# Attention stage of a two-layer fp32 hybrid block: hi products ahead of lo ones, an output-projection chunk between the last key transposes, the last biases loaded two steps ahead

## Chip, cores and metric

The kernel runs on 1 core of one Trainium2 chip. The metric is the device time of one execution in microseconds. Before the change it is 1264.56 us, the median of 3 runs (1263.3 to 1265.16).

## What is computed

A block of two layers works on 256 latent tokens and 256 context tokens of width 1024. Each layer is a half-step SwiGLU FFN, a token mixer and a second half-step FFN, and every one of these ends in a modulated, gated LayerNorm update. The mixer of layer 0, where the change is, is neighbourhood attention with 16 heads of 64: the latent queries see a window of the latent keys, with a relative bias and a mask, and all context keys, in one softmax.

```python
qkv = (hx @ w_qkv).reshape(B, S, 3, N_HEADS, HEAD_DIM)
q = apply_axial_rope(qkv[:, :, 0], rope)
k = apply_axial_rope(qkv[:, :, 1], rope)
v = qkv[:, :, 2]
...
s_win = jnp.where(mask, s_win + bias.astype(jnp.float32)[None], -jnp.inf)
s_ctx = jnp.einsum('bjqhd,bchd->bhjqc', q_r, k_c).astype(jnp.float32) * scale
p = jax.nn.softmax(jnp.concatenate([s_win, s_ctx], axis=-1), axis=-1).astype(v.dtype)
return (jnp.einsum('bhjqk,bjkhd->bjqhd', p[..., :nk], v_blk)
        + jnp.einsum('bhjqc,bchd->bjqhd', p[..., nk:], v_c))
...
y_lat = jnp.moveaxis(o, 0, 1).reshape(B, S, D) @ w_out
```

## The kernel before

**Hi and lo.** Every fp32 product is made of three. `split` (L110, L111) makes the hi part of a tile on ACT (a rounding copy) and then the lo part on DVE (source minus hi). A product of a and b is a_hi b_hi + a_hi b_lo + a_lo b_hi, with the three lines of `mmu` (L162, L163, L165) for the projections. A lo part is thus always ready one DVE instruction after its hi part.

**Who sets the order.** PE's instructions run in the order in which the program writes them. ACT, DVE, POOL and SP have their instructions placed by the tile framework's scheduler, from the same program and from priority offsets, so an edit of the program can move them too. Every engine takes its own list in order: an instruction that waits holds all behind it. Of the PSUM banks, transposes (`tpb`) share two, "mm" has three, "at" three.

**The attention stage** (about 465 to 585 us of the span). A loop of 32 steps goes over pairs of heads and two halves of the queries, `qt`. At every even step i, `scores` (L955 on) makes S for two heads at once (L962, three products for each), adds the bias tile (L966, DVE), takes the maximum (L968, DVE), the exponential (L970, ACT) and the scaling (L972, ACT), which gives `pr`. Two steps later `probs_T` transposes `pr` (L987, four 128x128 transposes into one bank PT) and splits the bank into pT hi and pT lo. One step after that, for the second half of the queries, `values` multiplies with v (L999 with the hi part, L1000 with the lo part, alternating, eight products) and sums into `osum` and `oT` (ACT and DVE).

**Fillers.** Between these, `fill_some` puts chunks of other products on PE: first the projections of keys, values and queries by quarters of the heads (`kv_quarter`, `q_half`), and from step 24 on the output projection `wo` of the heads that are done (`last_filler`). A wo chunk is one unit of six products; ten chunks are handed out by `islice(fin, 10)`, two of them of half a unit. The key transposes of a quarter (`rest`, L916 to L925) are two banks of four transposes, kT, and are made when a score needs them; those of the last quarter are made at step 24.

**Loads.** SP issues all loads of this stage in order. Each load waits until the one eight issues earlier has landed, and for its buffer. A bias tile takes two loads of 64 KB each (L874), from a table in which each row is read at another offset, and is then masked on POOL (L878). There are four bias buffers, and `bias_pair` for step i+2 is called at step i. The weights of the output projection, wor, come in 512 KB loads into four buffers that all projections share.

Of the kernel before, what the change touches and what calls it, by code (L numbers as in the profile page):

```python
# [9 lines left out]
F32 = mybir.dt.float32  # L10
# [6 lines left out]
P = 128  # L17
# [14 lines left out]
PB = {"mm": 3, "at": 3, "tp": 2}  # L32
W_EARLY = 40
ADA_SLOW, ADA_FAST = 3, 0.6
ADA_LATE = 20
ADA_LAG = 1
LN_EARLY = 60
# [31 lines left out]
def backbone_kernel(  # L69
# [6 lines left out]
    nc = tc.nc  # L76
# [9 lines left out]
    hp = phase.__enter__()  # L86
# [6 lines left out]
    def nm(s):  # L93
        uid[0] += 1
        return f"{s}_{uid[0]}"
# [10 lines left out]
    def tpb(s="tp"):  # L106
        return bank("tp", s)
# [358 lines left out]
    def run(gen):  # L466
        for _ in gen:
            pass
# [224 lines left out]
    steps = ((0, 1), (1, 1), (2, 2), (4, 2), (6, 2))  # L693
# [151 lines left out]
    def rtile(n):  # L845
        if n == 256:
            return hp.tile([P, n], F32, tag="kr", bufs=8, name=nm("kr"))
        return sp.tile([P, n], F32, tag="s2", bufs=S2, name=nm("qr"))
# [16 lines left out]

    BIAS = {}

    def bias_pair(h, qt):


        for hh in (h, h + 1):
            bt = hp.tile([P, 4, 64], F32, tag="bias", bufs=4, name=nm("bias"))
            for i in range(2):
                bias_dma[:] = [sync.dma_start(bt[64 * i:64 * i + 64],  # L874
                                              bass.AP(na_rpb_rev.tensor,
                                                      na_rpb_rev.offset + hh * 465 + (7 - 2 * qt - i) * 31 - 48,
                                                      [[1, 64], [31, 4], [1, 64]]))]
            nc.gpsimd.tensor_tensor(out=bt, in0=bt, in1=win_sb[:, ::-1].unsqueeze(1).to_broadcast([P, 4, 64]),  # L878
                                    op=ALU.add)
            BIAS[hh, qt] = bt[:, :, ::-1]  # L880
# [19 lines left out]
    def kv_quarter(g, res):  # L900
        krs, v = [], []

        def each(t, bk):
            if t < 2:
                krs.append(roped(bk[:, 0:256], t, 1, 4))
            else:
                r1 = rtile(256)
                nc.scalar.activation(r1, bk[:, 0:256], AF.Copy)
                krs.append(r1)
            v.append(act(F32R, "v"))  # L910
            z = v[t].rearrange("p (h s d) -> p h s d", h=4, s=2)
            split(bk[:, 256:512].rearrange("p (h d) -> p h d", h=4), z[:, :, 0], z[:, :, 1])

        yield from tile_panel(D + g * 256, 2 * D + g * 256, [hTs[t] for t in range(4)], "wkv", each)

        def rest():  # L916
            kT = []
            for j in range(2):
                ps = tpb("kT")
                for t in range(4):  # L920
                    nc.tensor.transpose(ps[:, t * P:(t + 1) * P], krs[t][:, j * P:(j + 1) * P], ident)
                hi, lo = act(F32R, "kTh"), act(F32R, "kTl")
                split(ps, hi, lo)
                kT.append((hi, lo))
            return kT  # L925

        res.append((Late(1, rest), v))
# [64 lines left out]
    def values(h):  # L992

        pth, ptl = PT.pop(h)
        ps = mmb("o", h == NH - 1)[:, 0:256]
        s = slice(h % 4 * P, (h % 4 + 1) * P)
        v = KV[h // 4][1]
        for k in range(4):
            nc.tensor.matmul(ps, v[k][:, s], pth[:, k], start=k == 0, stop=False)  # L999
            nc.tensor.matmul(ps, v[k][:, s], ptl[:, k], start=False, stop=k == 3)  # L1000
        if h % 2 == 0:
            osum[0] = sp.tile([P, 512], F32, tag="tmp", bufs=3, name=nm("osum"))[:, 0:256]
        p0 = h % 2 * 64
        t = osum[0][p0:p0 + 64]
        o_ins[h] = [nc.scalar.activation(t, ps[64:128], AF.Copy),
                    nc.vector.tensor_tensor(out=t, in0=ps[0:64], in1=t, op=ALU.add)]
        if h % 2:
            if len(oT) <= h // 4:
                oT.append([hp.tile([P, 512], F32R, tag="oT", bufs=6, name=nm("oT")) if len(oT) < 3 else act(F32R, "oT")
                           for _ in range(2)])  # L1010
            cs = slice((h // 2 % 2) * 256, (h // 2 % 2) * 256 + 256)
            last_o[:] = split(osum[0], *(z[:, cs] for z in oT[h // 4]))
# [34 lines left out]
    def fill_some(n):  # L1047
        for _ in range(n):
            if next(fill, 0) == 0:
                break  # L1050

    fill_some(A_PRE)
    for i in range(len(steps) + LAG + V_LAG):
# [4 lines left out]
                    sync.dma_start(xscr[t * P:(t + 1) * P, h * 512:(h + 1) * 512], xt[t][h])  # L1058
        while i + AHEAD < len(steps) and len(KV) <= steps[i + AHEAD][0] // 4:
            fill_some(1)  # L1060
        if i < len(steps) and i % 2 == 0:
            with tc.high_priority(offset=S_EARLY):
                prs[i], prs[i + 1] = scores(*steps[i])
            if i % 2 == 0 and i + 2 < len(steps):
                bias_pair(*steps[i + 2])
        credit += rate[min(i, len(rate) - 1)]
        n = int(credit)
        credit -= n
        if i >= 24 and fin is None:
            run(fill)  # L1070
            fin = last_filler()
            fill = islice(fin, 10)
        fill_some((n + 1) // 2)
        if i == len(steps) + LAG - 1:
            run(fill)
# [146 lines left out]
```

## Time and profile before

| | before |
|---|---|
| median of 3 runs | 1264.56 us (1263.3 to 1265.16) |
| profiled execution | 1262.04 us, span 1260.2 us |
| TensorE clock granted | full, in all 40 slices of the page |
| PE busy | 1242.7 us, 99% of the span |
| DVE, ACT, POOL busy | 950.1, 589.2, 41.5 us |
| chain that ended last | PE 90%, ACT 3%, DVE 3%, DMA 2% |

The profile is of one execution. In the timeline a line gives the start, the busy time, the engine, the line of the kernel, output and inputs, the number of instructions joined in the row, and in brackets the idle time ahead of it with the instruction that ended the idle time. Products on PE overlap, so the busy time of one is longer than the distance to the next start; distances of starts are used below.

### The profile page before, as it was taken

How to read it: one execution, taken by the hardware profiler on the slowest of the kernel's cores; microseconds unless marked ns; L12 is line 12 of the kernel's file. 1: busy time of each engine (PE TensorE's matmuls, PEld its weight loads, DVE VectorE, ACT ScalarE, POOL GpSimd, SP SyncE). 2: the span in 40 equal slices, each digit the busy share in tenths (PEclk: the TensorE clock that was granted, in tenths of full speed). 3: DMA queues.
4: the chain of work that ended last, by engine and by line, in shares of the span. 5: the costliest groups of instructions: out<-in, count | busy, mean ns of one | idle time of the engine just before them, and what ended most of it. 6: DMA issues, size and time to landing. Idle time of an engine off the chain costs nothing.

```text
span 1260.2 us, 17282 instructions
## 1 busy us (share of the span) xinstructions
PE 1242.7 (99%) x5910; PEld 1004.2 (80%) x5910; DVE 950.1 (75%) x1678; ACT 589.2 (47%) x1152; POOL 41.5 (3%) x71
## 2 busy tenths in 40 slices
PE   8999999999999999989999999999999999999997
PEld 5787778777878877867888788888788887888786
DVE  3699987888868877789889546988546788976546
ACT  2432132312326456687655435655435744655431
POOL 0000000000001111121000000000000000000000
PEclk9999999999999999999999999999999999999999
DMA  9976678788842744464899645898645764886641
GB/s 308 299 240 220 197 241 291 254 269 281 284 137 85 218 92 92 93 148 147 263 321 338 221 146 168 278 341 275 213 146 170 245 204 131 270 282 184 228 152 55
DMA packets 202776, 268.59 MB, mean 213 GB/s; under 512 B 30090, under 2 KB 149362, under 8 KB 202688
## 3 DMA queue, kind: packets, MB, share of 16 engines
q1 hardware_dynamic: 202652, 267.48, 67.2%
q8 instruction: 46, 0.75, 0.2%
q14 instruction: 42, 0.34, 0.1%
q10 hardware_dynamic: 36, 0.02, 0.0%
HBM read 265.27 MB, written 2.17 MB: 212 GB/s over the span
## 4 chain that ended last, share of the span: by engine, by line
PE 90%; ACT 3%; DVE 3%; DMA 2%; issue 1%; SPq 0%; POOL 0%; DVEq 0%; ACTq 0%
PE f L677 19%; PE w L162 17%; PE w L165 17%; PE w L163 17%; PE wkv L162 2%; PE wkv L163 2%; PE wkv L165 2%; PE wc L162 2%; PE wc L165 2%; PE wc L163 2%; PE gT L485 1%; DMA ar<-in_ada_w_dram 1%; PE ada L325 1%; PE hT L419 1%; PE S L962 1%
## 5 line engine op out<-in xcount | busy, mean ns | idle before, releaser
L208 ACT ACTIVATE w1h<-w1r 128x512 fp32r<-128x512 f32 (+1 forms) x352 | 199.9, 620 | 183.6 <-DMA w1r<-in_ffn_w_in_dram 63.5
L211 DVE TENSOR_TENSOR w1l<-w1r,w1h 128x512 fp32r<-128x512 f32 (+1 forms) x352 | 222.8, 678 | 49.2 <-ACT w1h L208 47.6
L162 PE MATMUL w<-w1h,hTh 128*128 128x512 f32 x528 | 209.4, 397 | 0.9 <-ACT hTh L110 0.9
L163 PE MATMUL w<-w1l,hTh 128*128 128x512 f32 x528 | 206.0, 390 | 0.2 <-DVE w1l L211 0.2
L294 DVE SCALAR_TENSOR_TENSOR acc<-ar,cst,acc 128x512 f32<-128x512 f32 x266 | 186.0, 745 | 14.5 <-DMA ar<-in_ada_w_dram 14.3
L162 PE MATMUL w<-w2h,gh 128*128 128x512 f32 (+1 forms) x446 | 173.4, 389 | 0.0
L163 PE MATMUL w<-w2l,gh 128*128 128x512 f32 (+1 forms) x446 | 172.1, 386 | 0.0
L211 DVE TENSOR_TENSOR w2l<-w2r,w2h 128x512 fp32r<-128x512 f32 x176 | 114.3, 687 | 76.3 <-ACT w2h L208 75.5
L208 ACT ACTIVATE w2h<-w2r 128x512 fp32r<-128x512 f32 x176 | 101.6, 624 | 145.4 <-PE w L165 101.6
L165 PE MATMUL w<-w1h,hTl 128*128 128x512 f32 x528 | 163.2, 390 | 0.3 <-DVE hTl L111 0.2
L165 PE MATMUL w<-w2h,gl 128*128 128x512 f32 (+1 forms) x446 | 136.0, 386 | 0.0
L677 PE MATMUL f<-h0h,w1h 128*128 128x512 f32 x352 | 132.8, 393 | 1.0 <-ACT w1h L208 0.6
L677 PE MATMUL f<-h0l,w1h 128*128 128x512 f32 x352 | 133.2, 391 | 0.0
L677 PE MATMUL f<-h0h,w1l 128*128 128x512 f32 x352 | 132.7, 390 | 0.0
L162 PEld LDWEIGHTS w<-w1h,hTh 128*128 128x128 f32 x528 | 99.2, 188 | 23.8 <-ACT hTh L110 1.7
L165 PEld LDWEIGHTS w<-w1h,hTl 128*128 128x128 f32 x528 | 98.9, 188 | 22.4 <-DVE hTl L111 1.5
L163 PEld LDWEIGHTS w<-w1l,hTh 128*128 128x128 f32 x528 | 99.2, 188 | 20.2 <-DVE w1l L211 0.6
L162 PEld LDWEIGHTS w<-w2h,gh 128*128 128x128 f32 x446 | 83.8, 188 | 19.3 <-issue 1.7
L163 PEld LDWEIGHTS w<-w2l,gh 128*128 128x128 f32 x446 | 83.8, 188 | 16.5
L165 PEld LDWEIGHTS w<-w2h,gl 128*128 128x128 f32 x446 | 83.3, 188 | 17.1
L677 PEld LDWEIGHTS f<-h0h,w1h 128*128 128x128 f32 x352 | 65.5, 188 | 19.4 <-issue 4.2
L677 PEld LDWEIGHTS f<-h0l,w1h 128*128 128x128 f32 x352 | 65.6, 188 | 14.3 <-issue 1.0
(184 smaller groups left out, 1697.3 us busy)
## 6 DMA issues: line engine op xcount, KB each, us to landing
w1r<-in_ffn_w_in_dram SPq DMA_DIRECT2D x340, 256.0 KB
ar<-in_ada_w_dram SPq DMA_DIRECT2D x128, 512.0 KB
w2r<-in_ffn_w_out_dram SPq DMA_DIRECT2D x88, 512.0 KB
ar<-in_ada_w_dram SPq DMA_DIRECT2D x32, 256.0 KB
wkvr<-in_na_w_qkv_dram SPq DMA_DIRECT2D x32, 256.0 KB
wcr<-in_sc_w_in_dram SPq DMA_DIRECT2D x32, 256.0 KB
wqr<-in_na_w_qkv_dram SPq DMA_DIRECT2D x8, 512.0 KB
bias<-in_na_rpb_dram SPq DMA_DIRECT2D x64, 64.0 KB
```

What stands on the lines that cost most here:

```text
L162: nc.tensor.matmul(ps, lh, rh, start=first and i == 0, stop=False)
L163: nc.tensor.matmul(ps, lh, rl, start=False, stop=False)
L165: nc.tensor.matmul(ps, ll, rh, start=False, stop=last and i == n - 1)
L208: nc.scalar.activation(hi[:, a:a + m // W_HI], raw[:, a:a + m // W_HI], AF.Copy)
L211: nc.vector.tensor_tensor(out=lo[:, a:b], in0=raw[:, a:b], in1=hi[:, a:b].bitcast(F32), op=ALU.subtract)
L294: nc.vector.scalar_tensor_tensor(out=a, in0=src, scalar=sc, in1=a, op0=ALU.mult, op1=ALU.add)
L325: nc.tensor.matmul(ps[32 * j:32 * j + 32, :], ones, acc[i][h], start=True, stop=True)
L419: nc.tensor.transpose(ps[:, k * P:(k + 1) * P], z[h][:, k * P:(k + 1) * P], ident)
L485: nc.tensor.transpose(ps[:, j * 256 + i * P:j * 256 + (i + 1) * P], g[:, j * P:(j + 1) * P], ident)
L677: nc.tensor.matmul(ps, w, hT0[k][part == 1], start=(k == part == 0), stop=(k == KC - 1 and part == 1))
L962: nc.tensor.matmul(banks[i], (qh, qh, ql)[f][ps, qs], (kh, kl, kh)[f][ps, :], start=f == 0, stop=f == 2)
```

## The change

The diff, with the two helpers' other lines cut:

```diff
+BIAS_AT = 24
...
-    def bias_pair(h, qt):
+    def bias_pair(h, qt, last=False):
         for hh in (h, h + 1):
-            bt = hp.tile([P, 4, 64], F32, tag="bias", bufs=4, name=nm("bias"))
+            if last:
+                bt = rtile(256).rearrange("p (a b) -> p a b", a=4)
+            else:
+                bt = hp.tile([P, 4, 64], F32, tag="bias", bufs=4, name=nm("bias"))
...
         def rest():
             kT = []
             for j in range(2):
+                if j and g == 3:
+                    fill_some(1)
                 ps = tpb("kT")
...
-        for k in range(4):
-            nc.tensor.matmul(ps, v[k][:, s], pth[:, k], start=k == 0, stop=False)
-            nc.tensor.matmul(ps, v[k][:, s], ptl[:, k], start=False, stop=k == 3)
+        for part, p in enumerate((pth, ptl)):
+            for k in range(4):
+                nc.tensor.matmul(ps, v[k][:, s], p[:, k], start=k == part == 0, stop=part == 1 and k == 3)
...
+        if i == BIAS_AT:
+            bias_pair(*steps[i + 2])
+            bias_pair(*steps[i + 4], True)
+            run(fill)
+            fin = last_filler()
+            fill = islice(fin, 10)
         if i < len(steps) and i % 2 == 0:
             with tc.high_priority(offset=S_EARLY):
                 prs[i], prs[i + 1] = scores(*steps[i])
-            if i % 2 == 0 and i + 2 < len(steps):
-                bias_pair(*steps[i + 2])
+        if i % 2 == 0 and i != BIAS_AT and (j := i + (2 if i < BIAS_AT else 4)) < len(steps):
+            bias_pair(*steps[j], i > BIAS_AT)
         credit += rate[min(i, len(rate) - 1)]
         n = int(credit)
         credit -= n
-        if i >= 24 and fin is None:
-            run(fill)
-            fin = last_filler()
-            fill = islice(fin, 10)
         fill_some((n + 1) // 2)
```

1. `values` makes its four products with the hi part first, then the four with the lo part, for all 16 heads.
2. Between the two banks of key transposes of the last quarter stands one wo chunk. For this the output projection is opened ahead of the scores of step 24. Ten chunks are handed out as before, so each later chunk moves one place forward.
3. The biases of step 28 are loaded at step 24 and those of step 30 at step 26, into tiles of the "kr" kind (the roped keys' buffers, of which there are eight), whose first use is over, in place of the "bias" buffers.

**The order on PE at the last key transposes** (step 24). PT and kT are banks of transposes, S the scores, wo the output projection, oT its left side. Before:

```order
L987 MATMUL PT_5180<-ident,pr_5075 128x128 x4
L921 MATMUL kT_5187<-ident,kr_4815 128x128
L921 MATMUL kT_5187<-ident,kr_4882 128x128
L921 MATMUL kT_5187<-ident,kr_4960 128x128
L921 MATMUL kT_5187<-ident,kr_5093 128x128
L921 MATMUL kT_5196<-ident,kr_4815 128x128
L921 MATMUL kT_5196<-ident,kr_4882 128x128
L921 MATMUL kT_5196<-ident,kr_4960 128x128
L921 MATMUL kT_5196<-ident,kr_5093 128x128
L962 MATMUL S_5205<-kTh_5192,qTh_4781 128x512
L962 MATMUL S_5206<-kTh_5192,qTh_4781 128x512
L962 MATMUL S_5205<-kTl_5193,qTh_4781 128x512
```

With the change:

```order
L927 MATMUL kT_5203<-ident,kr_4815 128x128
L927 MATMUL kT_5203<-ident,kr_4882 128x128
L927 MATMUL kT_5203<-ident,kr_4960 128x128
L927 MATMUL kT_5203<-ident,kr_5093 128x128
L163 MATMUL wo_5237<-woh_5230,oT_4327 128x512
L164 MATMUL wo_5237<-wol_5231,oT_4327 128x512
L163 MATMUL wo_5237<-woh_5230,oT_4327 128x512
L164 MATMUL wo_5237<-wol_5231,oT_4327 128x512
L166 MATMUL wo_5237<-woh_5230,oT_4328 128x512 x2
L927 MATMUL kT_5244<-ident,kr_4815 128x128
L927 MATMUL kT_5244<-ident,kr_4882 128x128
L927 MATMUL kT_5244<-ident,kr_4960 128x128
```

What moved: six wo products stand between the two kT banks, and no longer behind the scores; the scores follow the second bank at once in both.

**The order on PE at the end of the loop.** woh and wol are hi and lo of one unit of output weights, o the value sums. Before:

```order
L987 MATMUL PT_5549<-ident,pr_5415 128x128 x4
L162 MATMUL wo_5427<-woh_5496,oT_5174 128x512
L163 MATMUL wo_5427<-wol_5497,oT_5174 128x512
L162 MATMUL wo_5427<-woh_5496,oT_5174 128x512
L163 MATMUL wo_5427<-wol_5497,oT_5174 128x512
L165 MATMUL wo_5427<-woh_5496,oT_5175 128x512 x2
L987 MATMUL PT_5562<-ident,pr_5477 128x128 x4
L162 MATMUL wo_5260<-woh_5570,oT_5529 128x512
L163 MATMUL wo_5260<-wol_5571,oT_5529 128x512
L165 MATMUL wo_5260<-woh_5570,oT_5530 128x512
L987 MATMUL PT_5580<-ident,pr_5484 128x128 x4
L999 MATMUL o_5587<-pT_5509,v_4821 128x256
```

With the change:

```order
L166 MATMUL wo_5396<-woh_5455,oT_5175 128x512 x2
L993 MATMUL PT_5555<-ident,pr_5430 128x128 x4
L163 MATMUL wo_5237<-woh_5563,oT_5543 128x512
L164 MATMUL wo_5237<-wol_5564,oT_5543 128x512
L166 MATMUL wo_5237<-woh_5563,oT_5544 128x512
L993 MATMUL PT_5573<-ident,pr_5498 128x128 x4
L993 MATMUL PT_5580<-ident,pr_5505 128x128 x4
L1006 MATMUL o_5587<-pT_5523,v_4821 128x256
```

What moved: the chunk that stood between the last three transposes of probabilities is gone but for half a unit, and the last two PT stand side by side.

**The order on SP** behind the loads of the biases of step 24. wor is a load of output weights, x, gate and mrow belong to the LayerNorm update that follows. Before:

```order
L874 DMA bias_5150<-in_na_rpb_dram 64x4x64 x2
L203 DMA wor_5569<-in_na_w_out_dram 128x2x512
L874 DMA bias_5227<-in_na_rpb_dram 64x4x64 x2
L874 DMA bias_5231<-in_na_rpb_dram 64x4x64 x2
L358 DMA mrow_5247<-scr_116 8x128 x2
L358 DMA mrow_5247<-in_ln_g_dram 8x128
L358 DMA mrow_5247<-in_ln_b_dram 8x128
L203 DMA wor_5612<-in_na_w_out_dram 128x2x512
```

With the change, the rows up to the same two loads of output weights (ahead of the first row here stand, behind bias_5150, four loads into kr tiles, four biases and two x):

```order
L1039 DMA x_5216<-xscr 128x512
L1039 DMA x_5218<-xscr 128x512
L344 DMA gate_5220<-scr_116 128x512
L344 DMA gate_5222<-scr_116 128x512
L359 DMA mrow_5224<-scr_116 8x128 x2
L359 DMA mrow_5224<-in_ln_g_dram 8x128
L359 DMA mrow_5224<-in_ln_b_dram 8x128
L878 DMA kr_5352<-in_na_rpb_dram 64x4x64 x2
L878 DMA kr_5356<-in_na_rpb_dram 64x4x64 x2
L204 DMA wor_5562<-in_na_w_out_dram 128x2x512
L204 DMA wor_5612<-in_na_w_out_dram 128x2x512
```

What moved: the load of the unit behind bias_5150 (wor_5569 before, wor_5562 with the change) goes from the first place behind those biases to the 23rd, behind 12 bias loads, four x, two gate and four mrow.

On ACT three things move with it: the sum of one head (osum_5121) is now taken ahead of the scaling of pr_5068; the exponentials of the next scores stand ahead of the key split kTh_5208; and the first half of the split woh_5563<-wor_5562 stands ahead of pT_5374<-PT_5440 and of the two exponentials behind it. On DVE a half of wol_5362 stands ahead of the key split kTl_5209, both halves of wol_5456 ahead of pT_5155<-PT_5289, and one half of wol_5511 ahead of pT_5375<-PT_5440.

## Rows read from the trace of the kernel before

**Rows 1.** The page's part 1, busy time and number of instructions of each engine:

```profile
PE 1242.7 (99%) x5910; PEld 1004.2 (80%) x5910; DVE 950.1 (75%) x1678; ACT 589.2 (47%) x1152; POOL 41.5 (3%) x71
```

**Rows 2.** Windows of the stage: length, each engine's busy time, PEclk, DMA share, GB/s:

```profile
540.00:560.00 20.00, 16.71 (x103) 12.72 (x103) 18.96 (x42) 17.39 (x39) 4.35 (x6) 1.00 0.74 180
560.00:580.00 20.00, 19.28 (x116) 15.33 (x115) 16.87 (x40) 18.03 (x39) 2.88 (x4) 1.00 0.49 112
580.00:600.00 20.00, 18.83 (x88) 14.13 (x89) 18.15 (x33) 13.23 (x28) 2.34 (x5) 1.00 0.60 179
```

**Rows 3.** Timeline of PE around the last key transposes:

```profile
543.21 0.39 PE L999 MATMUL o<-pT,v 128*128 128x256 f32 x1 [0.75 <-ACT pT L110]
544.15 0.38 PE L1000 MATMUL o<-pT,v 128*128 128x256 f32 x1 [0.56 <-DVE pT L111]
544.38 0.28 PE L999 MATMUL o<-pT,v 128*128 128x256 f32 x1
544.50 0.28 PE L1000 MATMUL o<-pT,v 128*128 128x256 f32 x1
...
546.07 0.66 PE L987 MATMUL PT<-ident,pr 128*128 128x128 f32 x4
...
548.53 0.66 PE L921 MATMUL kT<-ident,kr 128*128 128x128 f32 x4 [0.42 <-DVE pT L111]
550.75 0.66 PE L921 MATMUL kT<-ident,kr 128*128 128x128 f32 x4 [1.56 <-DVE pT L111]
551.33 0.50 PE L962 MATMUL S<-kTh,qTh 64*128 64x512 f32 x2
551.74 0.50 PE L962 MATMUL S<-kTl,qTh 64*128 64x512 f32 x2
...
552.40 0.50 PE L162 MATMUL wo<-woh,oT 128*128 128x512 f32 x1
...
553.90 0.60 PE L987 MATMUL PT<-ident,pr 128*128 128x128 f32 x4
```

**Rows 4.** Timeline of ACT in the same stretch:

```profile
544.83 0.76 ACT L972 ACTIVATE pr<-pr,mx 128x512 f32<-128x512 f32 x1
545.62 0.38 ACT L1005 ACTIVATE osum<-o 64x256 f32<-64x256 f32 x1
...
554.54 0.60 ACT L110 ACTIVATE pT<-PT 128x512 fp32r<-128x512 f32 x1 [1.40 <-PE PT L987]
```

**Rows 5.** Timeline of DVE in the same stretch:

```profile
551.67 1.27 DVE L211 TENSOR_TENSOR wol<-wor,woh 128x512 fp32r<-128x512 f32 x2
...
555.32 0.68 DVE L111 TENSOR_TENSOR pT<-PT,pT 128x512 fp32r<-128x512 f32 x1
```

**Rows 6.** Timeline of PE at the later waits of the loop:

```profile
567.11 0.60 PE L987 MATMUL PT<-ident,pr 128*128 128x128 f32 x4
567.46 0.36 PE L999 MATMUL o<-pT,v 128*128 128x256 f32 x1
568.12 0.39 PE L1000 MATMUL o<-pT,v 128*128 128x256 f32 x1 [0.29 <-DVE pT L111]
...
578.67 0.38 PE L1000 MATMUL o<-pT,v 128*128 128x256 f32 x1 [0.42 <-DVE pT L111]
...
582.59 0.50 PE L162 MATMUL wo<-woh,oT 128*128 128x512 f32 x1 [0.23 <-ACT oT L110]
```

**Rows 7.** Issues on SP's queue (SPq), from the timeline:

```profile
539.87 0.38 SPq L203 DMA_DIRECT2D wor<-in_na_w_out_dram  x1
...
546.08 0.37 SPq L203 DMA_DIRECT2D wor<-in_na_w_out_dram  x1
...
556.83 5.31 SPq L874 DMA_DIRECT2D bias<-in_na_rpb_dram  x8
```

**Rows 8.** Windows around two loads of output weights, columns as in Rows 2:

```profile
541.00:543.00 2.00, 1.46 (x11) 1.08 (x9) 2.00 (x5) 2.00 (x6) 0.46 (x1) 1.00 0.73 258
...
548.00:551.00 3.00, 1.02 (x8) 0.68 (x7) 2.59 (x6) 2.95 (x8) 0.48 (x2) 1.00 0.84 198
```

## Prediction

> **What bounds the kernel now.** I read the page's busy times first: PE is busy for 1242.7 us, 99% of the span [rows 1]. So the time is PE's own work, and an edit pays only where PE stands still, or where it makes PE stand still. The windows show where that is. In 540 to 600 us PE is busy for 16.71, 19.28 and 18.83 us of 20, which leaves 3.29 + 0.72 + 1.17 = 5.18 us, and DVE is busy for 18.96 us in the first of them [rows 2]. That sum is a roof on any gain of this change, since it moves nothing elsewhere. Over the whole span of 1260.2 us PE lacks only 17.5 us, so little is left behind the stage to take up a delay, and what is won or lost here carries to the end. The timeline of PE then names the holes. The largest is the second bank of key transposes, 1.56 us of waiting for the lo half of a pT, since the two transpose banks are shared and a bank comes free only when DVE has read it [rows 3]. Beside it three value sums wait between their first hi and their first lo product, 0.56, 0.29 and 0.42 us [rows 3, 6], one waits 0.75 us for its hi part, and the first kT 0.42 us [rows 3].
>
> Three prices recur. A wo chunk takes 1.50 us (552.40 to 553.90) [rows 3]. Value products follow each other by 0.12 us (544.38 to 544.50) [rows 3]. A transpose bank is free again 2.10 us after its transposes start, when nothing is in the way: PT at 553.90, its hi part on ACT at 554.54 (ACT had waited for it), its lo part on DVE at 555.32 for 0.68 us, so 556.00 [rows 3 to 5]. Whatever DVE puts ahead of the lo part is added; a half of a wol costs it 0.64 us (1.27 for two) [rows 5].
>
> **The change, part by part.**
>
> *Hi products first.* The work of PE is the same: the same eight products per head, each with its own weight load, as before (5910 products, 5910 loads [rows 1]). The lo part is now wanted three products later, 3 x 0.12 = 0.35 us. Where the lo part is late PE gains at most that: 0.35 of the 0.56 at 544.15, and all of 0.29 and 0.35 of 0.42 at the later two. The Trainium skill, page "TensorE: Matmul & The Clock Gate", section "Step-by-step: what each phase is for", speaks against this part: a weight may be loaded once and used for many products, and the new order parts the two products that share v. By that rule 64 loads would be added, and at 0.17 us each (1004.2 / 5910 [rows 1]) the sum would have up to 10.9 us more where none is hidden; the trace disagrees, as the old order already pays one load per product, and the sum has nothing for it.
>
> At 544.15 the gain does not survive. On ACT the sum osum_5121 now stands ahead of the scaling of pr_5068. In the trace that scaling runs from 544.83 to 545.59 and the sum, 0.38, behind it [rows 4]. With the sum first the scaling ends at 545.9 to 546.1, while PE, 0.35 earlier, wants the transposes of this pr at 545.72 instead of 546.07 [rows 3]. So 0.2 to 0.55 us come back there. I take 0.35 - 0.55 = **0.2 us lost**.
>
> *A chunk between the last key transposes.* The second kT began 2.22 us after the first (548.53, 550.75), and four transposes need 0.35 (567.11 to 567.46) [rows 3, 6]: a hole of 1.87 us. The chunk of 1.50 us fills most of it, and is the same work taken from behind. What is late next are the scores: they follow the second kT at once and need hi and lo of the first. ACT now has two exponentials ahead of kTh, and DVE a wol half ahead of kTl. Before, S with kTh and S with kTl stood at 551.33 and 551.74 without a wait [rows 3]; the half of a wol puts kTl back by 0.64 [rows 5], the second exponential kTh by a like time, of which the end of the chunk hides a part. I take a wait of 0.2 on kTh and 0.5 on kTl. Bounds: none (both hidden), or 1.3 (both in full). 1.5 - 0.6 is **0.9 us gained**, between 0.2 and 1.5.
>
> Behind the scores, PT_5311 uses the bank of PT_5289, with one chunk between: 0.35 + 1.50 = 1.85 us behind it. The bank needs 2.10 with nothing in the way, so at least 0.25, and both halves of a wol now stand ahead of the lo part on DVE, up to 1.27 [rows 5] and thus at most 1.5. DVE starts the halves before the hi part is there, so I take half of them: **0.65 us lost**. Before there was no wait at this place.
>
> *The wo chunks one place forward.* mcT now takes the second bank behind PT_5440, so PT_5468 uses the same bank with a chunk and the one small transpose mcT between: 0.35 + 1.50 and a little, some 2.0 us, against 2.10 + 0.64 for the half wol on DVE. That is a wait of 0.7 in place of the hole at 568.12, 0.66 from the product before where 0.12 to 0.2 is usual: 0.5 [rows 6]: **0.2 us lost**, 0 to 0.4. At the end PT_5580 reuses the bank of PT_5555 with half a chunk (0.75) and one PT (0.35) between, 1.45 us against 2.10: 0.65 us of wait (bounds 0, if DVE and ACT run ahead, and 1.3, if a wol half comes between). The half chunk wants the oT of the sum that ends one chunk before it, which before came later: 0.4 us (0 to 0.8). The two value sums behind wait 0.15 each; the last wo, which waited 0.23 at 582.59 [rows 6], waits some 0.2 more. Against that stands the 0.42 at 578.67, some 0.6 with the restart that follows a wait, gone [rows 6]. Sum 0.65 + 0.4 + 0.3 + 0.2 - 0.6 = **0.95 us lost**.
>
> *Biases.* POOL's and DVE's work on them is the same. Earlier biases cost nothing by themselves. They move the load of a wo unit: before it was issued at 546.08 [rows 7], now behind 22 more loads. From 546.08 to 562.14 SP issued 24 loads [rows 7], 0.67 us each, so the new issue is at 546.08 + 22 x 0.67 = 560.8. The two loads before landed within 3.1 us (issued 539.87, the burst over by 543) and 4.9 us (issued 546.08, over by 551) [rows 8]: 563.9 to 565.7. Wanted it is at about 567: ACT has its split ahead of the pT hi of the transposes that stood at 567.11, whose hi is due 0.64 us later, less one split of 0.6 [rows 4, 6]. So nothing is lost, by 1.3 to 3 us of room. The bound below is nothing; the one above is the second rival. The Trainium skill, page "DMA: Bandwidth & Descriptors", section "Bandwidth", gives 0.95 us for a 64 KB transfer; as an estimate from that page the 12 bias loads one after another would take 3.4 us more than 0.67 each, and the load would land at 567.3 to 569.1.
>
> Sum: 0.2 - 0.9 + 0.65 + 0.2 + 0.95 = **1.1 us slower**, 0.1% of the time. The terms come from one execution of 1262.04 us, which is 2.5 us below the median of the runs, 1264.56; against its own time the sum gives 1263.1, against the median **1265.7**. A measurement of this kernel can tell about 0.2%, 2.5 us, from no change, so I forecast no change that can be told.
>
> **The rivals.**
>
> *The gains hold and the new waits do not appear.* Hi-first gives its full 0.35 three times and the chunk its 1.5, and ACT and DVE, which run their lists earlier when PE does, absorb the rest: -2.55, about **1262.0**. For it: 5.18 us are there to be had [rows 2], and in most of the new waits the bound below is nothing or a quarter of a us. Against it: DVE is full in the first window (18.96 of 20), so a lo part can hardly come earlier, and the bank time of 2.10 us is longer than what now stands between several transposes. For more than 0.2% nearly all of it must hold: 0.13.
>
> *The late load of output weights holds ACT (slower).* Place: woh_5563 ahead of pT_5374<-PT_5440 and of the two exponentials behind. Price: every us that the load lands after 567 keeps the hi part, the next free bank and the softmax of the last steps back by a us, and PE has one chunk (1.5) of cover, mostly used up. It decides from a landing at about 568.4, where 1.1 + 1.4 passes 2.5. With 0.83 us per issue in place of 0.67 the issue is at 564.3 and the landing at 567.4 to 569.2, +1.5 to +3.3; **1267.2** in the middle, and 1269 if the new waits are at their upper bounds besides. For it: SP's loads wait for landings, and 12 bias loads now stand ahead. Against: the same 24 loads before, with as many biases among them, kept 0.67. Some 0.25 for more than 2.5 us.
>
> *The order of PE does not decide.* DVE's list sets the pace through the stage, and PE waits as long as before at other places: 0, **1264.6**. For it speaks DVE's 18.96 of 20; against, that DVE is down to 16.87 in the next window [rows 2]. It lies within the same bounds as my forecast.
>
> **How the numbers follow.** My forecast with the third rival, all within 0.2%, has 0.61; faster by more has 0.13, slower by more 0.26. Unequal bounds reach from -2.6 (all gains) to +4.5 (late load with larger waits). For 8 in 10 I leave out the last tenth at both ends: 1262.6 to 1268.4.
>
> **What would show it.** Right: the wait of the second kT gone, the hi-to-lo holes in `values` down to 0.2 or less, and new waits of PT on pT lo of 0.5 to 0.8 us at two or three places, the last between two adjacent PT; PE busy in 540 to 600 us about a microsecond lower than before if the end of the stage is taken as the mark. Wrong on the side of rival one: no wait of PT on DVE over 0.3 us. Wrong on the side of rival two: woh behind a DMA wait on ACT at about 567, with PE idle over 1 us behind it.

## The result, and the profile after

The kernel with the change takes **1266.54 us** (median of 21 executions, 1265.27 to 1267.41) beside 1263.76 us (1262.42 to 1267.28) of 21 executions of the kernel before: a ratio of 1.0022, with a 95% interval of 1.0014 to 1.0027, 2.8 us slower. The forecast was 1265.7 in a range of 1262.6 to 1268.4. The time lies in it, but above the forecast, and the forecast was of no change that can be told, where this one is clear of noise. The forecast's own mechanism was at work, and the second rival on top of it.

The profiled execution of the changed kernel takes 1267.03 us, 4.99 more than that of the kernel before. The program reaches the stage 0.78 us later (the first value product at 543.99 for 543.21 [rows 3]), so times below are compared after taking 0.78 off. From that product to the wo behind the last wait it is 43.61 us (543.99 to 587.60), before 39.38 (543.21 to 582.59 [rows 3, 6]): 4.23 us longer.

First the windows of the stage in the changed kernel (columns as in Rows 2), the three of [rows 2] and then the middle one in pieces:

```profile
540.00:560.00 20.00, 17.23 (x105) 12.53 (x103) 18.55 (x40) 17.94 (x40) 6.34 (x8) 1.00 0.67 146
560.00:580.00 20.00, 17.54 (x95) 13.71 (x94) 14.36 (x35) 13.10 (x29) 1.74 (x2) 0.91 0.55 148
580.00:600.00 20.00, 18.07 (x90) 13.48 (x89) 17.98 (x33) 14.29 (x32) 1.27 (x3) 1.00 0.39 114
...
560.00:562.00 2.00, 2.00 (x13) 1.69 (x12) 2.00 (x5) 0.38 (x1) 0.00 (x0) 1.00 0.48 46
562.00:564.00 2.00, 2.00 (x14) 1.82 (x14) 1.11 (x4) 1.95 (x6) 0.00 (x0) 1.00 0.45 26
...
566.00:568.00 2.00, 2.00 (x12) 1.46 (x11) 1.82 (x4) 1.19 (x3) 0.22 (x1) 1.00 0.85 259
568.00:570.00 2.00, 1.56 (x7) 0.98 (x6) 1.33 (x3) 0.00 (x0) 1.01 (x1) 1.00 0.89 326
570.00:572.00 2.00, 0.00 (x0) 0.00 (x0) 0.72 (x2) 1.87 (x5) 0.00 (x0) 1.00 0.39 133
572.00:574.00 2.00, 1.98 (x12) 1.98 (x12) 1.97 (x5) 2.00 (x5) 0.00 (x0) 0.65 0.07 24
574.00:576.00 2.00, 2.00 (x9) 1.03 (x8) 1.01 (x2) 1.20 (x3) 0.00 (x0) 0.50 0.49 151
576.00:578.00 2.00, 2.00 (x12) 1.69 (x13) 1.96 (x5) 0.57 (x1) 0.00 (x0) 1.00 0.91 293
```

The first window gained half a microsecond of PE time. The loss is in the second: PE 17.54 for 19.28, and its clock is below full speed. The pieces show a hole in which PE does nothing in 570 to 572, ACT nothing in 568 to 570, and behind it a clock of 0.65 and 0.50. The timeline of PE in the changed kernel names the waits:

```profile
546.84 0.66 PE L993 MATMUL PT<-ident,pr 128*128 128x128 f32 x4 [0.26 <-ACT pr L978]
...
549.33 0.66 PE L927 MATMUL kT<-ident,kr 128*128 128x128 f32 x4 [0.43 <-DVE pT L112]
...
551.20 0.60 PE L927 MATMUL kT<-ident,kr 128*128 128x128 f32 x4
...
551.97 0.50 PE L968 MATMUL S<-kTh,qTh 64*128 64x512 f32 x2 [0.17 <-ACT kTh L111]
...
552.87 0.50 PE L968 MATMUL S<-kTl,qTh 64*128 64x512 f32 x2 [0.40 <-DVE kTl L112]
...
557.56 0.66 PE L993 MATMUL PT<-ident,pr 128*128 128x128 f32 x4 [0.54 <-DVE pT L112]
...
568.95 0.61 PE L166 MATMUL wo<-woh,oT 128*128 128x512 f32 x2
572.02 0.66 PE L993 MATMUL PT<-ident,pr 128*128 128x128 f32 x4 [2.46 <-DVE pT L112]
572.43 1.94 PE L1006 MATMUL o<-pT,v 128*128 128x256 f32 x8
574.30 0.79 PE L968 MATMUL S<-kTh,qTh 64*128 64x512 f32 x2
...
577.77 1.19 PE L1006 MATMUL o<-pT,v 128*128 128x256 f32 x8
578.80 0.40 PE L163 MATMUL wo<-woh,oT 128*128 128x512 f32 x1
...
582.81 0.63 PE L993 MATMUL PT<-ident,pr 128*128 128x128 f32 x4 [0.54 <-DVE pT L112]
...
587.60 0.50 PE L163 MATMUL wo<-woh,oT 128*128 128x512 f32 x1 [0.57 <-ACT oT L111]
```

The second key transposes no longer wait (551.20; 1.56 before [rows 3]). Against that stand waits that were not there before, 0.17, 0.40, 0.54, 0.54, and one of 2.46 us. Follow that one back over three engines. It ended when DVE had made a lo part, for which DVE had waited for the hi part on ACT:

```profile
571.27 0.69 DVE L112 TENSOR_TENSOR pT<-PT,pT 128x512 fp32r<-128x512 f32 x1 [1.95 <-ACT pT L111]
```

On ACT the hi part stands behind the split of a unit of output weights, which waited 2.94 us for its load:

```profile
566.05 1.14 ACT L209 ACTIVATE woh<-wor 128x512 fp32r<-128x512 f32 x2
570.13 0.63 ACT L209 ACTIVATE woh<-wor 128x512 fp32r<-128x512 f32 x1 [2.94 <-DMA wor<-in_na_w_out_dram]
570.66 0.58 ACT L111 ACTIVATE pT<-PT 128x512 fp32r<-128x512 f32 x1
```

And SP had issued that load, one of the two at 561.57, directly behind four bias loads:

```profile
558.89 2.58 SPq L878 DMA_DIRECT2D kr<-in_na_rpb_dram  x4
561.57 1.07 SPq L204 DMA_DIRECT2D wor<-in_na_w_out_dram  x2
562.74 3.77 SPq L188 DMA_DIRECT2D w1r<-in_ffn_w_in_dram  x2
```

The issue, 561.57 less 0.78, is at the forecast's 560.8. The landing is not: ACT's wait ended at 570.13, 8.6 us after the issue, where the forecast had 3.1 to 4.9. For the first 3 us little moves (46 and 26 GB/s with the DMA engines half busy, in 560 to 564): the trace's packets of 256 bytes, the rows of the biases, fill this time, and the first of 2048 bytes, the rows of the weights, starts at 565.25. Then the weights of both loads come, with those of the two FFN loads behind them, at 259 and 326 GB/s.

The 2.46 us cost more than themselves in this execution. Behind them the granted clock is at its lower level, 1.2 GHz, for about 3.4 us (0.65 in 572 to 574, 0.50 in 574 to 576): the eight value products at 572.43 need 1.87 us to the next start, those at 577.77 need 1.03. From the transposes at 572.02 to the wo at 578.80 it is 6.78 us; with the load early, the first experiment, the same products need 5.31 at full clock. The clock cost 1.5 us.

### The profile page after: what moved, and what is told of

Read it like the earlier page. It is cut to its first block, busy times and chain, and to the rows that moved or that the text cites. A ratio compares the mean times of both kernels' runs of the same rounds, so it can differ in the third digit from the quotient of the medians.

```text
span 1265.2 us, 17275 instructions
## 1 busy us (share of the span) xinstructions
PE 1246.1 (98%) x5910; PEld 1006.8 (80%) x5910; DVE 951.3 (75%) x1678; ACT 589.6 (47%) x1152; POOL 41.6 (3%) x71
## 4 chain that ended last, share of the span: by engine, by line
PE 90%; DMA 3%; DVE 3%; ACT 2%; SPq 1%; issue 1%; POOL 0%; DVEq 0%; ACTq 0%
PE f L678 18%; PE w L163 17%; PE w L166 17%; PE w L164 17%; PE wkv L163 2%; PE wkv L164 2%; PE wkv L166 2%; PE wc L163 2%; PE wc L166 2%; PE wc L164 2%; DMA ar<-in_ada_w_dram 2%; PE gT L486 1%; PE ada L326 1%; PE S L968 1%; PE hT L420 1%
```

## Experiments

Three causes had to be parted: the late load; the waits that the forecast had summed; and TensorE's clock, which no term of the sum had held. All edits are against the changed kernel. Twelve kernels ran; eleven were timed beside the kernel before, whose median was 1263.88 (35 executions) for the first four, 1264.33 (33) for the next four, 1264.35 (27) for the three after.

**The loads of output weights early.** The edit raises the priority of these loads. On ACT one exponential and its scaling then stand ahead of the split of the second key bank, and DVE's list moves with them; the rest of the order is that of the changed kernel.

```diff
-        with tc.high_priority(offset=w_early[0]):
+        with tc.high_priority(offset=w_early[0] + (30 if s == "wo" else 0)):
```

> The whole change, but with the load of the output weights wor_5562 issued in the middle of the biases of step 26 again (about 550 us) and not behind the last ones. Theory A (the late load holds ACT, PE stands 2.5 us for PT_5468 and then runs 3 us at half its clock): no DMA wait ahead of woh_5563, PT_5468 waits 0.6 to 0.9 us, the granted clock stays 1.00 in 560 to 580 us, and the time is 1.0 to 1.4 us above the kernel before, ratio 1.0003 to 1.0012. Theory B (the two shared transpose banks set the loss; the load only comes on top of a wait that is there anyway): PT_5468 still waits over 2 us for the lo part, ratio 1.0018 or more.

1263.70 us, ratio 0.9997 (0.9989 to 1.0006). The unit's load is issued at 547.77, and ACT waits for no load. Timeline of PE, at the place of the 2.46 us and at the end:

```profile
568.75 0.66 PE L992 MATMUL PT<-ident,pr 128*128 128x128 f32 x4 [0.37 <-DVE pT L111]
...
574.06 0.40 PE L162 MATMUL wo<-woh,oT 128*128 128x512 f32 x1
...
576.69 0.50 PE L162 MATMUL wo<-woh,oT 128*128 128x512 f32 x1 [0.64 <-ACT oT L110]
...
578.63 0.63 PE L992 MATMUL PT<-ident,pr 128*128 128x128 f32 x4 [0.54 <-DVE pT L111]
...
583.42 0.50 PE L162 MATMUL wo<-woh,oT 128*128 128x512 f32 x1 [0.57 <-ACT oT L110]
```

The late load is the loss: without it the 2.8 us are gone. The stage from the same value product (542.83) to 583.42 takes 40.59 us, 1.21 more than the 39.38 of before, where the forecast's sum said 1.1; the execution takes 1262.90, where the sum gave 1263.1 against its own time. Yet the median is that of the kernel before, below the ratio of 1.0003 to 1.0012 that was expected. So the sum was right between these two profiles, and wrong as a difference of medians; the last experiment bears on why.

**The load ahead of the last four biases only.**

```diff
-            bias_pair(*steps[j], i > BIAS_AT)
...
+            with tc.high_priority(offset=-30 if i > 24 else 0):
+                bias_pair(*steps[j], i > 24)
```

> The whole change with the four loads of the last biases put behind the two loads of output weights; PE's and ACT's lists are those of the change. In the change the two were issued at 561.6 and the first landed at 570.1, 8.5 us later, where loads that did not stand behind biases took 3 to 5. Theory A1 (the four bias loads ahead in the queue make most of these 8.5 us): issued at about 559, landed by 565, no DMA wait on ACT, ratio 0.9997 to 1.0008. Rival A2 (the two loads and the two w1r loads behind them share the engines, so 1.5 MB have to go by first): landed at 567 to 568, a wait of 0 to 1 us on ACT, ratio 1.0008 to 1.0016.

1264.15 us, ratio 0.9998 (0.9989 to 1.0007); no instruction's place on PE or ACT differs from the changed kernel's, and on DVE one half of a wol moves ahead of a maximum. Its first value product is at 544.36, and the weights are issued at 559.27, 14.9 us behind it (17.6 in the changed kernel); the four bias loads now follow them and the two FFN weight loads. Its windows, where the changed kernel has 46 and 26 GB/s:

```profile
560.00:562.00 2.00, 2.00 (x12) 1.38 (x11) 1.68 (x5) 0.48 (x2) 0.00 (x0) 1.00 0.69 229
562.00:564.00 2.00, 2.00 (x17) 1.82 (x16) 1.43 (x4) 1.75 (x4) 0.00 (x0) 1.00 1.00 359
```

And the split on ACT waits for PE to give its buffer back, no longer for a load:

```profile
568.04 0.63 ACT L208 ACTIVATE woh<-wor 128x512 fp32r<-128x512 f32 x1 [0.21 <-PE wo L165]
```

The issue is 2.7 us sooner, about the time of four bias issues (2.58). That alone would bring the landing from 8.6 to 5.9 us behind the old issue; but the weights now move at once and not after 3 us of little traffic. The last packet of 2048 bytes is through at 564.50, so both loads have come 5.2 us behind the issue of the first, with the same two FFN loads behind them. So the bias loads ahead in the queue hold up more than their own issue, and sharing with the other loads does not explain the 8.6 us.

**The late unit's rounding on POOL, its load as late as in the change.**

```diff
-                nc.scalar.activation(hi[:, a:a + m // W_HI], raw[:, a:a + m // W_HI], AF.Copy)
+                if pool:
+                    nc.gpsimd.tensor_copy(hi[:, a:a + m // W_HI], raw[:, a:a + m // W_HI])
+                else:
+                    nc.scalar.activation(hi[:, a:a + m // W_HI], raw[:, a:a + m // W_HI], AF.Copy)
```

Here `pool` is true for the seventh wo unit, the late one.

> The whole change with the load as late as it is there, but the hi half of that one unit (woh_5563) is rounded on POOL and not on ACT, so that the late load has nothing behind it on ACT. Theory A (it is the place at the head of ACT's list, not the lateness by itself): the load still lands at about 569 to 570, ACT shows no DMA wait, PT_5468 waits under 1 us in place of 2.5, the clock stays 1.00, and the time is 0 to 1.5 us above the kernel before, ratio 1.0000 to 1.0012. Rival (the late load costs through the products that need it, or through DVE's lo half, which now waits for POOL): ratio 1.0018 or more.

1264.89 us, ratio 1.0004 (0.9995 to 1.0012). POOL begins its rounding as late as ACT did:

```profile
569.90 1.37 POOL L213 CAST woh<-wor 128x512 fp32r<-128x512 f32 x2 [0.21 <-ACT pr L982]
```

ACT waits for no load and the clock stays full, and most of the loss is gone with the load still late. So it was ACT's list behind the split that turned the late load into time. It missed on one point: the transposes still waited 1.54 us, not under 1, since the scheduler now put an exponential on ACT and two halves of another wol on DVE ahead of their bank's split.

**The parts by themselves.** Bias ahead undone (hi-first and chunk):

```diff
-            bias_pair(*steps[i + 2])
-            bias_pair(*steps[i + 4], True)
...
+            if i % 2 == 0 and i + 2 < len(steps):
+                bias_pair(*steps[i + 2])
```

> Hi products first and the chunk between the key transposes, with the biases loaded two steps ahead left out. Theory A: the load of wor_5562 stands early, so no DMA wait ahead of its split; PT_5303 (the second PT behind the scores of step 24) waits 1.6 us, PT_5468 0.7, and the time is 1.0 to 1.5 us above before, ratio 1.0005 to 1.0013. Theory B: as the change, ratio 1.0018 or more.

1264.47 us, ratio 1.0004 (0.9995 to 1.0012), just under the 1.0005 to 1.0013 expected. No late load; three transposes wait for pT, 1.95, 0.52 and 0.53 us.

The chunk undone (hi-first and bias ahead):

```diff
-                if j and g == 3:
-                    fill_some(1)
```

with the output projection opened behind the scores again, as before.

> Hi products first and the biases two steps ahead, with the chunk between the key transposes left out. The load of the same unit is as late as in the change (behind the last biases), but its split stands five transposes later on ACT. Theory A: it is the two together that cost; here the load may land at 569 without holding anything, clock 1.00, time 0 to 0.5 us above before, ratio 0.9995 to 1.0007. A rival to A (the late load costs wherever it is used): ratio 1.0015 or more, PE idle over 1 us behind a wait for a DMA.

1263.96 us, ratio 1.0001 (0.9992 to 1.0009). Bias loads are ahead as in the change, yet no wait for a load: without the chunk ahead, the late unit's split stands later on ACT. The load is also a little sooner here, 15.4 us behind the first value product and not 17.6.

Hi-first alone (both of these undone):

> Hi products ahead of lo ones alone. Theory A: 0.35 us less at each of three value sums, the second kT waits 0.75 in place of 1.56 us since on DVE the sum of a head now stands behind the lo part that frees the bank, PT_5156 waits 0.5 us, S 0.4 us: 0.7 us below before, ratio 0.9990 to 1.0000. A rival (the order of the value sums gives nothing, the lo parts only wait elsewhere): ratio 1.0000 to 1.0006.

1263.58 us, ratio 1.000 (0.999 to 1.001). The second kT waits 0.54 where it waited 1.56, but a value sum waits 1.07 at 569.10: DVE, which makes the lo part, had waited 0.74 and 0.27 us for POOL's masks on bias tiles that had landed late. Loading the biases ahead would spare that wait. The ratio does not part the two theories, which met at 1.0000.

Bias ahead alone (hi-first and chunk undone):

> Biases two steps ahead alone; the load of the same unit stands behind the last biases, its split stands late on ACT. Theory A: no DMA wait on ACT, second kT still waits 1.6 us, ratio 0.9998 to 1.0008. Rival (the bias loads cost by themselves): 1.0015 or more.

1265.26 us, ratio 1.0008 (0.9999 to 1.0016). The second kT waits 1.56 as before, S behind it 0.88, then the clock is at 0.50 for 3.4 us. The load is issued late (560.16), its split stands at 573.57, and nothing waits for it.

The chunk alone:

> The chunk between the key transposes alone. Theory A: the wait of the second kT goes from 1.56 to 0.3 us, new waits of PT of 1 us behind the scores, 0.4 to 0.7 at PT_5468 and 0.5 at the last PT, together 0.5 to 1.3 us above before, ratio 1.0002 to 1.0011; no clock drop. Rival (the chunk is a gain that the rest of the change gives back): 0.9985 to 0.9995.

1264.28 us, ratio 1.0001 (0.9992 to 1.001). The waits of transposes for pT are 0.82, 0.47 and 0.54. Against the expectation the clock drops to 0.50, at 546.6, ahead of all of them and behind the holes of the first value sum (0.76 and 0.56).

None of the parts costs 0.2% alone or with hi-first. The loss needs bias ahead **and** the chunk: the first makes the load late, the second brings its split forward on ACT, ahead of a pT that PE soon wants.

**One chunk fewer at step 26.** The chunk between the key transposes stays, but one is held back at step 26, so the chunks behind, and with them the late unit's split, are where they were before. The load stays late.

```diff
-        n = int(credit)
-        credit -= n
+        n = int(credit) - (i == 26)
+        credit -= n + (i == 26)
```

> The whole change, its load of output weights as late as there, but one chunk fewer is handed out at step 26, so that from there on every chunk, and the split of the late unit, stands where it stood before the change. Theory A (the chunk between the key transposes costs only because all later chunks move forward, which brings the split of the late load ahead of pT on ACT): no DMA wait on ACT though the load lands at 568 to 570, PT_5468's wait and the wait between two adjacent PT gone, PT_5311 still waits 0.5 us, clock 1.00 through 540 to 600 us; 1 to 2 us below the change and 0 to 2 us below before, ratio 0.9984 to 1.0000. Rival (the late load or the bias loads cost in themselves): ratio 1.0010 or more.

**1262.03 us** (11 executions, 1261.35 to 1263.13), ratio **0.9982 (0.9973 to 0.9991)**: faster than both kernels. The window in which the changed kernel has PE at 17.54:

```profile
560.00:580.00 20.00, 19.93 (x122) 15.87 (x122) 18.04 (x43) 18.70 (x40) 1.47 (x2) 1.00 0.55 148
```

The load is issued at 560.93 and brings 266 and 299 GB/s in 566 to 570, as late as in the changed kernel, but on ACT its split comes behind both hi parts and the exponentials, without a wait:

```profile
567.76 0.60 ACT L110 ACTIVATE pT<-PT 128x512 fp32r<-128x512 f32 x1
...
569.89 1.66 ACT L208 ACTIVATE woh<-wor 128x512 fp32r<-128x512 f32 x3
```

Of the three waits of transposes for pT that the forecast had (0.65, 0.7, 0.65), one is left (0.54, at 557.02). The stage takes 38.52 us (543.43 to 581.95), 0.86 less than before.

The same with the load early as well:

> As the run before, with the load of that unit issued early as in the first experiment. Theory A: the same time within 0.0005, since nothing waits for the load any more in either. Rival (a late load costs through shared DMA engines even where nothing waits for it): 0.0008 or more below the run before.

1261.59 us, ratio 0.9982 (0.9974 to 0.9991): the same. Where ACT has nothing urgent behind the split, the late load costs nothing.

And without bias ahead, one chunk fewer at step 24:

> Hi products first and the chunk between the key transposes, no biases ahead, one chunk fewer handed out at step 24. Theory A: no wait at the scores behind the key transposes, PT waits 0.9 us once; the bias add of the last scores waits for its load by up to 1 us, as with hi first alone; ratio 0.9986 to 1.0002. Rival (loading the biases two steps ahead is worth nothing): equal to the two runs before within 0.0004.

1261.66 us, ratio 0.998 (0.9971 to 0.9989). The two gaining parts are enough, with a value sum that waits 0.78 after DVE had waited 1.19 for the mask of a late bias. The rival held: the time is equal to the two above, so loading the biases two steps ahead brought nothing that can be measured here.

**The kernel before, profiled once more**, to see why its first profile (1262.04) is faster than its median:

> The kernel before, unchanged, profiled once more. The first profile of it shows 1262.04 us and a clock at its upper level in every slice; most of its other executions have a mean granted clock of 0.997 or 0.998 and a median near 1264. Theory C (most executions of the kernel before lose about 1.6 us to TensorE's clock right behind the hole of the second key transposes): this execution has a mean clock of 0.997 or 0.998, a window of some 3 us at 0.50 that begins within 2 us behind that hole (at 551 to 557 us), and a time of 1263 to 1265.5. Rival (the executions differ elsewhere, for instance at the start): the windows from 540 to 600 us are at the upper level as in the first profile, and where the mean clock is lower the stretch with 0.50 lies in another stage. If the mean clock is 0.999 again the run tells nothing apart.

1264.17 us, mean clock 0.997. Its windows (the same stretch was at 1.00 in the first profile):

```profile
544.00:546.00 2.00, 1.62 (x11) 1.43 (x13) 2.00 (x6) 1.98 (x6) 0.00 (x0) 0.93 0.61 35
546.00:548.00 2.00, 2.00 (x10) 1.35 (x9) 1.75 (x5) 1.45 (x4) 0.19 (x1) 0.50 0.64 69
548.00:550.00 2.00, 2.00 (x15) 2.00 (x14) 1.08 (x3) 1.53 (x4) 0.54 (x1) 0.72 0.72 199
```

The stage takes 41.30 us (543.43 to 584.73) and not 39.38. The drop is real and in this stage, but the place was wrong: it stands behind the holes of the first value sum (0.75 and 0.56, as in [rows 3]), not behind that of the second kT. It is not all of the 1.9 us either:

```profile
551.90 0.66 PE L921 MATMUL kT<-ident,kr 128*128 128x128 f32 x4 [1.61 <-DVE pT L111]
...
557.76 0.39 PE L1000 MATMUL o<-pT,v 128*128 128x256 f32 x1 [0.16 <-DVE pT L111]
...
570.27 0.38 PE L1000 MATMUL o<-pT,v 128*128 128x256 f32 x1 [0.83 <-DVE pT L111]
```

The second kT stands 8.47 us behind the first value product, 7.54 in the first profile: 0.9 us more. The other microsecond comes with two value sums that wait 0.16 and 0.83 for their lo part, at full clock, where [rows 6] have 0.29 for the second. Whether these waits follow from the drop is not shown.

The mean clocks of all executions say how often a drop comes. Of 35 executions of the kernel before, beside the first four kernels, by mean granted clock:

| mean clock | executions | mean time, us |
|---|---|---|
| 0.999 | 1 | 1262.34 |
| 0.998 | 10 | 1263.41 |
| 0.997 | 21 | 1264.35 |
| 0.996, 0.995 | 3 | 1265.48 |

The five profiles with a mean of 0.997 (the changed kernel, the chunk undone, bias ahead alone, the chunk alone, and this one) each have one such drop of 3.4 us in this stage; the nine with 0.999 have none ahead of the kernel's last 4 us, where PE has no more work and the clock is at its lower level in all of them. No profile is at 0.998: such an execution can be of either kind, since the stretch at the end, 2.1 to 4.2 us long in the profiles, moves the mean too. The first profile of the kernel before is of a rare kind: one of the 35 is at 0.999, and none is as fast as its 1262.04. With the load early, 8 of 11 executions are at 0.999 and 3 at 0.998; with one chunk fewer at step 26, 5 and 6.

## Why the prediction was right or wrong

**The sign.** The prediction named what would show it, and both kinds of sign came: those of its own sum (the second kT without a wait, holes of 0.21 between hi and lo, waits of 0.54 for pT, the last between two adjacent PT), and that of being wrong on the side of rival two: woh behind a DMA wait on ACT, with PE idle over 1 us behind it. So the range held the time, but the forecast of a change too small to be told did not: the sum had 1.1 us, measured are 2.8.

**The sum.** Nearly every term stood. In the changed kernel, forecast and measured: the wait on the scaling 0.2 to 0.55 (0.55 taken), 0.26; scores on kTh and kTl 0.2 and 0.5, 0.17 and 0.40; the transposes behind them 0.65, 0.54; the last pair of transposes 0.65, 0.54; the last wo 0.2 more than 0.23, 0.57. Two terms show only with the load early: the transposes behind mcT 0.7, 0.37; the half chunk on oT 0.4, 0.64. The sum of 1.1 was 1.21 there. That it came so near is in part luck: two of its terms do not follow from their own words. The chunk's 1.5 less waits of 0.2 and 0.5 is 0.8 and not 0.9, and 0.25 with half of 1.27 is 0.89 and not 0.65; put right, the sum is 1.4.

**The step that failed is the landing of the load**: "The two loads before landed within 3.1 us (issued 539.87, the burst over by 543) and 4.9 us (issued 546.08, over by 551) [rows 8]: 563.9 to 565.7." The issue was right to 0.1 us, the landing was 569.4 (570.13 less 0.78). The two loads taken as the price did not stand right behind biases: they were issued 3.8 and 1.8 us after the last bias ahead of them. The row to look for was a weight load right behind bias loads, and the trace of the kernel before has one, two loads of FFN weights behind eight biases, with its windows:

```profile
562.23 2.64 SPq L187 DMA_DIRECT2D w1r<-in_ffn_w_in_dram  x2
...
562.00:564.00 2.00, 2.00 (x14) 1.29 (x13) 1.15 (x4) 1.95 (x6) 0.00 (x0) 1.00 0.70 88
564.00:566.00 2.00, 2.00 (x12) 1.65 (x12) 1.29 (x4) 1.41 (x3) 1.42 (x2) 1.00 0.75 92
566.00:568.00 2.00, 1.83 (x11) 1.36 (x9) 2.00 (x5) 1.69 (x5) 0.73 (x1) 1.00 0.83 217
```

For 4 us only about 90 GB/s move there. With the load ahead of the last four biases the wait was gone. The prediction also had an estimate that came nearer. The Trainium skill, "DMA: Bandwidth & Descriptors", section "Bandwidth", gives the time of a 64 KB transfer, measured for loads issued from GpSimd, and the prediction estimated from that page a landing at 567.3 to 569.1; the trace's landing is 0.3 past the upper end. It is near in the number alone: the estimate spreads its 3.4 us over 12 bias loads, and in the trace the first weights come 3.7 us behind the issue, with four biases right ahead of it.

**Rival two** had the place, ACT's split ahead of a hi part, and the price, a microsecond for each one past 567. Its reason for the late landing, 0.83 us for each issue, did not come: the issues kept their 0.67. Landing at 569.4 it gives 1.1 + 2.4 = 3.5; the stage was 4.23 longer. The transposes waited 2.1 longer than with the load early (2.46 for 0.37), the half chunk's 0.64 went, as its oT was ready by then, and 1.5 came from the clock: 1.21 + 2.1 - 0.64 + 1.5 = 4.2. In this profile the clock is the term that the rival lacked. The loss of the median does not need it: the one execution of the changed kernel at 0.999 still takes 1266.27 us. That the load costs only through the split's place is shown by the late load that cost nothing once the split stood later.

**From profile to median.** The profiles differ by 4.99 us, the medians by 2.78. The prediction set its sum on the median as if every execution were like the profiled one, "2.5 us below the median". Those 2.5 us were no fixed offset. Some 0.8 of them was the base: 1264.56 is a median of 3, that of 21 is 1263.76, and on it the sum would have said 1264.9. So the time lies as near to the forecast of 1265.7 as it does partly by luck.

The rest goes largely with the clock. Of the 95 executions of the kernel before beside the first eleven kernels, 4 are at 0.999, with a mean of 1262.7 us; the 48 at 0.997 take 1264.4, 1.6 us more. With the load early 8 of 11 are at 0.999 and none at 0.997, and these 8 take 1263.6, 0.9 more than the 4 of before, near the sum. This fits a change that is slower by its sum and loses the clock less often, so that the medians come out equal. It is argued, not shown: the same 8 spread from 1262.22 to 1265.29, so executions differ by more than the clock. Nor is it shown which hole brings the drop. Hi-first alone leaves executions at 0.997 (4 of 12), the chunk alone too (4 of 11), both together as well (4 of 11); both together with one chunk held back at step 24 have none (of 11). That stays open.

**Hi-first.** The Trainium skill, "TensorE: Matmul & The Clock Gate", section "Step-by-step: what each phase is for", says that a weight can be loaded once and used for many products; by that the prediction had up to 10.9 us for weights loaded again. The traces disagree: the changed kernel has 5910 loads for 5910 products, as before, and hi-first alone has a ratio of 1.000 within 0.1%.

**The forecast of gains** (rival one, 1262.0) did not happen in this change, but it was to be had: one chunk held back at step 26 gives 1262.03. Two of the three waits for pT that the sum counted came from moving every later chunk forward, not from the chunk between the transposes.

## What to carry to other kernels

When an edit moves a load past others, price its landing by the loads that will stand ahead of it in the queue and not by its own kind elsewhere, and then look what stands behind its consumer on that engine: a late load is free until an urgent instruction is queued behind the one that waits for it. A chunk put into a hole is taken from somewhere; hold the rest of the order where it was, and the gain stays. Before a sum is set on a median, look whether the profiled execution is of the usual kind (here by the mean granted clock), since a hole can cost the clock as well as its own length.

## What the runs showed of the hardware

- TensorE's granted clock fell to 0.50 (1.2 GHz) for about 3.4 us behind holes of very different length: behind one of 2.46 us in the changed kernel, and behind two of 0.75 and 0.56 us in the second profile of the kernel before. In the first profile of that kernel the same two holes left the clock at 1.00.
- The first of two 512 KB loads issued behind four bias loads of 64 KB, in rows of 256 bytes, landed 8.6 us after its issue, and while those were under way the DMA engines were about half busy at 26 to 46 GB/s. Issued ahead of them, 229 and 359 GB/s moved in the same stretch, and both had come after 5.2 us.
